# Ten early first-layer blocks ahead of the gates, six more kept in DRAM, channel transposes spread, x loaded in one row: a hybrid SSD and PEER layer

## The chip, the core and the metric

The kernel runs on one core of a Trainium2 chip. Times are device microseconds (us) of that core, and a kernel's time is the median of its runs. The engines are TensorE (PE, with its weight loads PEld), VectorE (DVE), ScalarE (ACT), GpSimd (POOL) and SyncE (SP), which issues most transfers.

## What is computed

One decoder layer over 512 tokens and 16 meta tokens of width 1024, in float32. The mixer is a projection into SSD and short-conv channels, and a product with an output matrix. Behind it stands the PEER block: 128 x 128 experts, 8 heads that choose 16 each.

```python
proj = n @ w_in                                  # z, xbc, dt, sc_b, sc_c, sc_x
xbc = silu(causal_dwconv(xbc, conv_ssd_w) + conv_ssd_b)
y = ssd_scan(xs, dt, A, Bm, Cm) + d_skip * xs    # chunks of 128 tokens
h = h + concat([rmsnorm(y * silu(z)), sc_b * causal_dwconv(sc_c * sc_x)]) @ w_out
n = rmsnorm(h)                                   # PEER
s = einsum('thsd,hskd->thsk', n @ w_q, sub_keys)
experts, gates = product_key_top16(s)            # per token and head
act = gelu(einsum('td,tkd->tk', n, expert_u[experts])) * gates
h = h + einsum('tk,tkd->td', act, expert_v[experts])
out = rmsnorm(h)[16:]
```

## The kernel before

All float32 products run as three passes over operands split into a high half (a ScalarE copy, line 88) and a low half (a subtraction, line 90, on VectorE or on GpSimd). `Stream` does this for all weights, in one order: a weight tile is loaded, then split piece by piece (two pieces to a block) four pieces ahead of use, in a ring of 12 halves.

**The first stage.** Rows of x are loaded in two pairs, normalised (`x_stats`), and transposed (`x_pair`); the first two projections begin on the first pair alone. Then 20 channel tiles are projected (`xbc_tile`: TensorE, an eviction by ScalarE, a convolution in four VectorE operations, a Silu). Of every four x tiles five chunks of tokens are transposed back (`to_tok`, four PSUM buffers), after the second projection of the next four.

**The experts.** The PEER block is computed densely for the last 384 tokens: for each of 128 blocks of 128 experts a first layer (`z_unit`, line 709, 24 matmuls and a Gelu) and a second layer (`vmm`, line 1036, 18 matmuls). What scales the result are gates, a 128 x 128 table for every token, which is built from one-hot products (`gates`, 24 calls of 32 small matmuls) and written to DRAM. `select` makes lists of experts out of the top-k; it casts the index lists on GpSimd (line 816), works on VectorE and has the three lists transposed by TensorE (line 871). The first 128 tokens gather their experts row by row (`fetch`, `dot`, `weigh`, `addv`) during the block loop.

First-layer blocks need no gates. So some are computed early: the first `NR` = 22 stay in SBUF, and those in `SPILL` are written to DRAM (`zd`) and read back in the block loop. `EARLYZ` lists both, `NZ0` counts them, `ZSEL` of them are issued ahead of the first `select`, `ZLATE` behind the last gate, and the rest are spread over the 24 gates calls. The block loop (`z_next`, `h_unit`, `sparse_step`, `vmm`) computes the others, 22 blocks ahead of use. `ZPOOL` says of how many early blocks GpSimd subtracts both low halves; `XP` says it for the channel projections, with its first entry for the first tile.

The code is written in this order, but a scheduler decides how the instructions stand on each engine. Every engine works its row in order.

Of the kernel before, what the change touches and what calls it, by code (L numbers as in the profile page):

```python
# [6 lines left out]
F32 = mybir.dt.float32  # L7
# [4 lines left out]
AF = mybir.ActivationFunctionType  # L12
# [5 lines left out]
P = 128  # L18
# [4 lines left out]
NT = T // P  # L23
L = META + T
NXS = 12
NG = 4
# [6 lines left out]
NB = 128  # L33
# [4 lines left out]
TC = 16  # L38
XP = ((False, True), (True, True))
ZLATE = 5  # L40
# [5 lines left out]
NR = 22  # L46
SPILL = tuple(range(NR + 2, NB - 6, 7))
EARLYZ = tuple(range(NR)) + SPILL
NZ0 = len(EARLYZ)
ZSEL = 6  # L50
ZPOOL = 6
NW = 12
# [64 lines left out]
def layer_kernel(tc, x, meta, g_mix, w_xbc, w_dt, w_sc, w_z, conv_w, conv_b, dt_bias, a_log, d_skip,  # L117
                 norm_w, sc_w, w_out, g_ffn, g_ffn_row, w_q, keys, u_t, uv, g_final, out, stage=99):
    nc = tc.nc
    dma = nc.sync.dma_start  # L120
    act = nc.scalar.activation
# [3 lines left out]
    with ExitStack() as top:  # L125
        const = top.enter_context(tc.tile_pool(name="const", bufs=1))
        dram = top.enter_context(tc.tile_pool(name="dram", bufs=1, space=DRAM))
        small = top.enter_context(tc.tile_pool(name="small", bufs=6))
        stp = top.enter_context(tc.tile_pool(name="stp", bufs=1))

        h = const.tile([P, NT, D], F32, name="h_in", tag="hbc")
# [9 lines left out]
        gmix = const.tile([P, KD], F32, name="gmix")  # L141
        gffn = const.tile([P, KD], F32, name="gffn")
        warm = small.tile([P, 1], F32, name="ss")
        nc.gpsimd.memset(warm, 1.0)
        act(warm, warm, AF.Sqrt)
        dma(out=meta_t, in_=meta)
        dma(out=h[:, 0, :], in_=x[0:P, :])
        dma(out=gmix, in_=g_mix)
        dma(out=h[:, 1, :], in_=x[P:2 * P, :])

# [32 lines left out]
        for g in range(NG):  # L183
            add(("xbc", 12 + g), w_xbc[12 + g], pool=XP[0 if g == 0 else 1])
            if g == 0:
                add(("dt",), w_dt, 1, KD * NH)
        for j in [16, 17, 18, 19] + list(range(NXS)):
            add(("xbc", j), w_xbc[j], pool=XP[1])
        for g in range(NG):
# [17 lines left out]
        st = Stream(nc, tc, stp, items)  # L207
        st.load_upto(2)
        for tt in range(2, NT):
            dma(out=h[:, tt, :], in_=x[tt * P:(tt + 1) * P, :])  # L210
        st.load_upto(4)
# [66 lines left out]

        x_stats(0)

        def x_pair(pr):
# [10 lines left out]
        x_pair(0)  # L292
        x_stats(1)

# [90 lines left out]
        xs_tok = [ring6(f"xs_tok{c}") for c in range(5)]  # L385
        b_tok = mc.tile([P, 4, NG, P], F32, name="b_tok")
        bc = const.tile([P, 2, NG, L], F32, name="bc", tag="hbc")
        b_ch = bc[:, 0]
# [12 lines left out]

        def to_tok(srcs, dst, nch=5):
            for c in range(nch):
                t0, t1 = tok(c)
                n = t1 - t0
                p = psS.tile([P, 512], F32, name="pS")
                for i, s in enumerate(srcs):
                    nc.tensor.transpose(p[:n, i * P:(i + 1) * P], s[:, t0:t1], ident)
                nc.any.tensor_copy(out=dst(c)[:n], in_=p[:n])

# [4 lines left out]
        for g in range(2):  # L415
            xbc_tile(16 + g, c_ch[:, g, :])
        to_tok([b_ch[:, g, :] for g in range(NG)], lambda c: b_tok[:, c].rearrange("p g n -> p (g n)"), 4)
        for g in range(2, NG):
            xbc_tile(16 + g, c_ch[:, g, :])
        do_dt3()  # L420
        pend = None
        for jg in range(3):
            srcs = []
            for i in range(4):
                xc = w2(L)
                xbc_tile(jg * 4 + i, xc)
                srcs.append(xc)
                if i == 1 and pend is not None:
                    pend()
            pend = lambda srcs=srcs, jg=jg: to_tok(srcs, lambda c: xs_tok[c][:, jg * 512:(jg + 1) * 512])  # L430

# [147 lines left out]
        def zb0():  # L579
            pend()  # L580
            for g in range(NG):
                ssd_a(0, g)
                ssd_b(0, g)
# [71 lines left out]
        h = const.tile([P, NT, D], F32, name="h", tag="hbc")  # L655
# [466 lines left out]
```

## Time and profile before

| | us |
|---|---|
| median of 3 runs (1717.19 to 1719.57) | 1719.07 |
| profiled execution | 1718.36 |
| span of its instructions | 1716.7 |
| TensorE busy | 1667.3 |
| VectorE busy | 1330.8 |
| ScalarE busy | 777.0 |
| GpSimd busy | 575.0 |

The stages, in us from the span's start: start and channel projections until 163, the rest of the mixer until about 475, the PEER queries until 575.7, the first `select` until 620, the gates until 771, remaining early blocks until 800, the block loop until 1708.5, the output until 1716.7. In the profile "L90" is line 90 of the kernel before; a wait stands in brackets behind the instruction that waited, with what released it.

### The profile page before, as it was taken

What the parts mean: (1) busy time and instruction counts of PE and PEld (TensorE: products, weight loads), DVE (VectorE), ACT (ScalarE), POOL (GpSimd) and SP (SyncE); (2) the same over time, 40 slices, a digit from 0 to 9 for tenths busy, and PEclk for the clock granted to TensorE, in tenths of its full rate; (3) what the DMA queues carried; (4) which work ended last, traced back from release to release, by engine and by line L of the source; (5) the groups of instructions that cost most, each with busy time, mean ns of one, the idle gap of its engine ahead of it and who ended that gap; (6) DMA issues with size and microseconds to landing.
All of it is one profiled execution on the core that took longest, in us unless ns stands there. A gap on an engine that the chain in (4) does not pass through costs nothing.

```text
span 1716.7 us, 26803 instructions
## 1 busy us (share of the span) xinstructions
PE 1667.3 (97%) x9544; PEld 1508.2 (88%) x9544; DVE 1330.8 (78%) x2820; ACT 777.0 (45%) x1548; POOL 575.0 (33%) x544
## 2 busy tenths in 40 slices
PE   6999999999999979999999999999999999999998
PEld 5989998878788978989999999999999999999886
DVE  5766468897689999995777777777777777777888
ACT  6444443455543445664444444444444444444444
POOL 2442335440155500202333333333333333333442
PEclk9999999999999989999999999999999999999999
DMA  4221221135532238889888887887888888888762
GB/s 153 75 84 56 73 98 50 65 98 199 180 99 84 90 116 251 257 269 372 320 301 304 328 325 287 331 319 290 327 311 311 310 317 314 317 300 330 274 240 99
DMA packets 131387, 382.91 MB, mean 223 GB/s; under 512 B 10532, under 2 KB 65444, under 8 KB 112820
## 3 DMA queue, kind: packets, MB, share of 16 engines
q1 hardware_dynamic: 112244, 245.92, 42.4%
q0 software_dynamic: 18432, 134.23, 20.3%
q8 instruction: 75, 1.23, 0.3%
q10 hardware_dynamic: 576, 1.05, 0.2%
q14 instruction: 60, 0.49, 0.1%
HBM read 351.14 MB, written 30.02 MB: 222 GB/s over the span
## 4 chain that ended last, share of the span: by engine, by line
PE 76%; DVE 18%; issue 3%; ACT 2%; DMA 0%; POOL 0%; SPq 0%; DVEq 0%; ACTq 0%; POOLq 0%
PE pV L1036 30%; PE pZ L709 26%; PE pA L303 6%; PE pA L600 5%; PE pA L443 4%; DVE w L399 2%; DVE o L912 2%; DVE w L90 1%; PE pR L918 1%; DVE o L908 1%; DVE x L774 1%; DVE x L771 1%; DVE ssb L772 1%; ACT w L88 1%; PE pS L532 1%
## 5 line engine op out<-in xcount | busy, mean ns | idle before, releaser
L88 ACT ACTIVATE w<-raw 128x512 fp32r<-128x512 f32 (+1 forms) x657 | 407.7, 625 | 611.3 <-PE pV L1036 243.8
L709 PE MATMUL pZ<-n,w 128*128 128x384 f32 (+1 forms) x3408 | 659.5, 347 | 0.0
L709 PEld LDWEIGHTS pZ<-n,w 128*128 128x128 f32 x3408 | 606.8, 189 | 21.4 <-DVE w L90 0.2
L90 POOL TENSOR_TENSOR w<-raw,w 128x512 fp32r<-128x512 f32 x211 | 292.0, 1390 | 754.5 <-ACT w L88 740.6
L1036 PE MATMUL pV<-w,hh 128*128 128x512 f32 x2304 | 537.2, 389 | 0.0
L90 DVE TENSOR_TENSOR w<-raw,w 128x512 fp32r<-128x512 f32 (+1 forms) x446 | 308.5, 694 | 252.7 <-ACT w L88 251.1
L1036 PEld LDWEIGHTS pV<-w,hh 128*128 128x128 f32 x2304 | 431.2, 188 | 82.7
L303 PE MATMUL pA<-nT,w 128*128 128x256 f32 (+3 forms) x1488 | 207.8, 296 | 0.6 <-ACT w L459 0.4
L303 PEld LDWEIGHTS pA<-nT,w 128*128 128x128 f32 (+1 forms) x1488 | 192.2, 188 | 5.4 <-ACT w L459 0.5
L969 DVE SCALAR_TENSOR_TENSOR h<-row,a,h 128x1024 f32<-128x1024 f32 x128 | 165.2, 1290 | 0.1
L959 DVE SCALAR_TENSOR_TENSOR row<-row,n2k 128x1024 f32<-128x1024 f32 x128 | 161.4, 1263 | 0.6 <-DMA row<-in_uv,xid 0.6
L953 POOL DMA_INDIRECT row<-in_uv,xid x128 | 144.8, 1132 | 23.3 <-DVE a L965 5.5
L1007 DVE TENSOR_TENSOR hh<-hf,hh 128x384 fp32r<-128x384 f32 x128 | 103.4, 808 | 20.0 <-ACT hh L1006 19.8
L506 POOL TENSOR_TENSOR sr<-aS,ut 128x384 fp32r<-128x384 f32 x64 | 66.5, 1059 | 79.9 <-PE pS L508 41.5
L1004 DVE TENSOR_TENSOR hf<-zg,gt 128x384 f32<-128x384 f32 x128 | 81.3, 635 | 5.1 <-DMA gt<-gd 1.4
L1006 ACT ACTIVATE hh<-hf 128x384 fp32r<-128x384 f32 x128 | 65.5, 512 | 33.0 <-PE pV L1036 18.5
L921 ACT ACTIVATE stg<-pR 128x512 f32<-128x512 f32 x96 | 54.4, 599 | 39.3 <-PE pR L918 26.2
L443 PE MATMUL pA<-w,nT 128*128 128x384 f32 x384 | 72.2, 345 | 0.0
L443 PEld LDWEIGHTS pA<-w,nT 128*128 128x128 f32 x384 | 68.6, 192 | 1.6 <-issue 1.1
L788 ACT ACTIVATE zg<-pZ 128x384 f32<-128x384 f32 x128 | 61.0, 477 | 19.7 <-PE pZ L709 18.7
L918 PE MATMUL pR<-o,o 128*128 128x128 f16 x768 | 58.0, 222 | 6.1 <-DVE o L912 6.1
L912 DVE TENSOR_TENSOR o<-oag,ob 128x1024 f16<-128x1024 f16 x96 | 63.3, 695 | 0.0
(235 smaller groups left out, 1421.8 us busy)
## 6 DMA issues: line engine op xcount, KB each, us to landing
raw<-in_u_t SPq DMA_DIRECT2D x128, 512.0 KB, 4.8
raw<-in_uv SPq DMA_DIRECT2D x128, 512.0 KB, 4.9
gd<-stg SPq DMA_DIRECT2D x24, 1024.0 KB, 6.4
gt<-gd SPq DMA_DIRECT2D x16, 1536.0 KB, 9.8
raw<-in_w_out SPq DMA_DIRECT2D x32, 512.0 KB, 3.5
raw<-in_w_xbc SPq DMA_DIRECT2D x20, 512.0 KB, 3.5
raw<-in_w_q SPq DMA_DIRECT2D x16, 512.0 KB, 3.5
raw<-in_w_z SPq DMA_DIRECT2D x16, 384.0 KB, 3.0
```

What stands on the lines that cost most here:

```text
L88: nc.scalar.activation(hi, r, AF.Copy)
L90: ins = (nc.gpsimd if on_pool else nc.vector).tensor_tensor(lo, r, hi.bitcast(F32), ALU.subtract)
L303: mm(p[:m, :o1 - o0], wp[a][:, c0:c0 + m], nTs[b][:, k, o0:o1], start=i == 0, stop=i == 3 * KD - 1)
L443: mm(pz[tt][:, :GW], nTs[b][:, k, t0:t0 + P], wz[a], start=k == 0 and i == 0, stop=k == KD - 1 and i == 2)
L600: mm(po[pr, i, nh], ys[b], wp[a], start=kn == 0 and q == 0, stop=kn == 15 and q == 2)
L709: mm(ps[s][:, :o1 - o0], wp[a_][:, k * P:(k + 1) * P], n2s[b_][:, 4 * i + k, o0:o1], start=cnt[s] == 0, stop=cnt[s] == 23)
L912: V.tensor_tensor(o1, oag[:, t0 // 2:t0 // 2 + 2, :, None, :].broadcast_to([P, 2, 16, 16, 2]), ob[:, t0 // 2:t0 // 2 + 2, None, :, :].broa ...
L953: nc.gpsimd.indirect_dma_start(out=row.rearrange("p a d -> p (a d)"), out_offset=None, in_=uv, in_offset=bass.IndirectOffsetOnAxis(ap=xids ...
L959: V.scalar_tensor_tensor(row[:, 0], row[:, 0], 1.0, n2k[:, tt], ALU.mult, ALU.mult, accum_out=z)
L969: V.scalar_tensor_tensor(h[:, tt, :], row[:, 1], a, h[:, tt, :], ALU.mult, ALU.add)
L1007: V.tensor_tensor(hl, hf_, hh.bitcast(F32), ALU.subtract)
L1036: mm(acc[tt, nh], hp_[a][:, ts_], vp_[w], start=b == 0 and q == 0, stop=b == NB - 1 and q == 2)
```

## The change

`SPILL` takes every fifth block instead of every seventh: 20 blocks instead of 14 are kept in DRAM, 42 instead of 36 are early. `ZSEL` and `ZPOOL` go from 6 to 10. The rest of the early blocks (27 for 25) is spread over the gates, five come behind them. `to_tok` takes a list of chunks and is called three times, with two, two and one chunk, after the first, second and third projection of the next four tiles; its copies go to ScalarE, where the scheduler chose between two engines before. All four loads of x come ahead of the first weights, and both `x_stats` stand in one row. The first tile's first low half moves to GpSimd, and a Sqrt that did nothing but load ScalarE's table is gone. Line numbers of the new file are 5 lower from the middle on.

```diff
-XP = ((False, True), (True, True))
+XP = ((True, True), (True, True))
...
-SPILL = tuple(range(NR + 2, NB - 6, 7))
+SPILL = tuple(range(NR + 2, NB - 6, 5))
 EARLYZ = tuple(range(NR)) + SPILL
 NZ0 = len(EARLYZ)
-ZSEL = 6
-ZPOOL = 6
+ZSEL = 10
+ZPOOL = 10
...
-        warm = small.tile([P, 1], F32, name="ss")
-        nc.gpsimd.memset(warm, 1.0)
-        act(warm, warm, AF.Sqrt)
         dma(out=meta_t, in_=meta)
-        dma(out=h[:, 0, :], in_=x[0:P, :])
-        dma(out=gmix, in_=g_mix)
-        dma(out=h[:, 1, :], in_=x[P:2 * P, :])
+        for tt in range(NT):
+            dma(out=h[:, tt, :], in_=x[tt * P:(tt + 1) * P, :])
+            if tt == 0:
+                dma(out=gmix, in_=g_mix)
...
         st = Stream(nc, tc, stp, items)
-        st.load_upto(2)
-        for tt in range(2, NT):
-            dma(out=h[:, tt, :], in_=x[tt * P:(tt + 1) * P, :])
         st.load_upto(4)
...
         x_stats(0)
+        x_stats(1)
...
         x_pair(0)
-        x_stats(1)
...
-        def to_tok(srcs, dst, nch=5):
-            for c in range(nch):
+        def to_tok(srcs, dst, chunks):
+            for c in chunks:
...
-                nc.any.tensor_copy(out=dst(c)[:n], in_=p[:n])
+                act(dst(c)[:n], p[:n], AF.Copy)
...
-                if i == 1 and pend is not None:
-                    pend()
-            pend = lambda srcs=srcs, jg=jg: to_tok(srcs, lambda c: xs_tok[c][:, jg * 512:(jg + 1) * 512])
+                if i < 3 and pend is not None:
+                    pend((2 * i, 2 * i + 1)[:5 - 2 * i])
+            pend = lambda ch, srcs=srcs, jg=jg: to_tok(srcs, lambda c: xs_tok[c][:, jg * 512:(jg + 1) * 512], ch)
...
-            pend()
+            pend(range(5))
```

TensorE between the last query and the first gate, before. `pZ` with 384 columns is a first-layer block (24 matmuls), the line 871 transposes the lists, and `o` are one-hot factors:

```order
L765 MATMUL pR<-kt,qT 128x128 x4
L709 MATMUL pZ<-n_4669,w 128x384 x138
L871 MATMUL pR<-ident,lists 128x128 x3
L709 MATMUL pZ<-n_4669,w 128x384 x44
L918 LDWEIGHTS o_6749
L918 MATMUL pR<-o_6751,o_6749 128x128
```

And now:

```order
L760 MATMUL pR<-kt,qT 128x128 x4
L704 MATMUL pZ<-n_4666,w 128x384 x234
L866 MATMUL pR<-ident,lists 128x128 x3
L704 MATMUL pZ<-n_4666,w 128x384 x44
L913 LDWEIGHTS o_6894
L913 MATMUL pR<-o_6896,o_6894 128x128
```

Of first-layer matmuls 96 more, four blocks, stand ahead of the lists' transposes; behind them there are 44 as before.

GpSimd at the same place, before; `cand` are sums of candidates, `xT` is the cast of index lists and line 90 the subtraction of a low half:

```order
L90 TENSOR_TENSOR w<-raw,w 128x512
L733 TENSOR_TENSOR cand<-v_2_5090 128x64
L733 TENSOR_TENSOR cand<-v_3_5091 128x48
L733 TENSOR_TENSOR cand<-v_3_5091 128x64
L816 CAST xT<-x_1_5093 128x256
L90 TENSOR_TENSOR w<-raw,w 128x512 x4
L816 CAST xT<-x_2_5094 128x256
L816 CAST xT<-x_3_5095 128x256
L816 CAST xT<-x_0_5092 128x256
```

And now:

```order
L728 TENSOR_TENSOR cand<-v_2_5087 128x64
L728 TENSOR_TENSOR cand<-v_3_5088 128x48
L728 TENSOR_TENSOR cand<-v_3_5088 128x64
L811 CAST xT<-x_1_5090 128x256
L90 TENSOR_TENSOR w<-raw,w 128x512 x5
L811 CAST xT<-x_2_5091 128x256
L90 TENSOR_TENSOR w<-raw,w 128x512 x7
L811 CAST xT<-x_3_5092 128x256
L811 CAST xT<-x_0_5089 128x256
L862 COPY xg_6449<-lists 128x128
```

Four subtractions between the first and the second cast have become five, and seven stand between the second and the third.

VectorE's row at the start, before. The 16-row operations are the meta tokens' norm; `w,ss<-h_in` squares half a row of x:

```order
L265 SCALAR_TENSOR_TENSOR w_151,ss_146<-h_in 128x512
L225 RECIPROCAL rs_r<-rs_t 16x1
L265 SCALAR_TENSOR_TENSOR w_153,ss_146<-h_in 128x512
L226 TENSOR_TENSOR rs_t<-rs_r 16x1
L90 TENSOR_TENSOR w<-raw,w 128x512
L227 TENSOR_TENSOR rs_t<-rs_t,rs_v 16x1
L270 TENSOR_TENSOR ss_155<-ss_146 128x2
L228 TENSOR_SCALAR rs_t<-rs_t 16x1
L223 TENSOR_SCALAR rs_v<-ss_155 128x2
L229 TENSOR_TENSOR rs_r<-rs_r,rs_t 16x1
L240 TENSOR_SCALAR mn<-meta_t,rs_r 16x1024
L225 RECIPROCAL rs_r<-rs_t 128x2
```

And now:

```order
L260 SCALAR_TENSOR_TENSOR w_148,ss_143<-h_in 128x512
L220 RECIPROCAL rs_r<-rs_t 16x1
L260 SCALAR_TENSOR_TENSOR w_150,ss_143<-h_in 128x512
L221 TENSOR_TENSOR rs_t<-rs_r 16x1
L260 SCALAR_TENSOR_TENSOR w_171,ss_166<-h_in 128x512
L222 TENSOR_TENSOR rs_t<-rs_t,rs_v 16x1
L265 TENSOR_TENSOR ss_152<-ss_143 128x2
L260 SCALAR_TENSOR_TENSOR w_173,ss_166<-h_in 128x512
L223 TENSOR_SCALAR rs_t<-rs_t 16x1
L218 TENSOR_SCALAR rs_v<-ss_152 128x2
L265 TENSOR_TENSOR ss_175<-ss_166 128x2
L224 TENSOR_TENSOR rs_r<-rs_r,rs_t 16x1
```

The first low half is gone from it. Of two more squares (of the fourth row of x) one stands ahead of the first pair's sums (`ss_152`), one ahead of the variance (`rs_v`) made of them.

## Rows read from the trace of the kernel before

**Rows 1.** The page, part 1: busy time, share of the span, count of instructions.

```profile
PE 1667.3 (97%) x9544; PEld 1508.2 (88%) x9544; DVE 1330.8 (78%) x2820; ACT 777.0 (45%) x1548; POOL 575.0 (33%) x544
```

**Rows 2.** Busy us (count) of PE, PEld, DVE, ACT, POOL; granted clock, DMA share, GB/s.

```profile
600.20:620.00 19.80, 10.40 (x48) 9.65 (x47) 19.34 (x62) 2.99 (x7) 2.68 (x1) 0.83 0.25 80
...
620.00:771.10 151.10, 147.91 (x1307) 136.08 (x1306) 147.56 (x264) 95.89 (x176) 14.61 (x3) 0.98 0.81 240
...
800.20:1708.50 908.30, 908.30 (x4490) 818.12 (x4488) 690.37 (x1099) 382.67 (x798) 323.11 (x253) 1.00 0.82 301
```

**Rows 3.** Waits of TensorE, the longest: total us, times, longest.

```profile
PE pS L286 <- DVE rs_r L225: 12.9, 1, 12.9
```

**Rows 4.** Timeline, TensorE, ahead of the gates: start us, us, operation, [idle before, releaser].

```profile
575.71 24.62 PE L709 MATMUL pZ<-n,w 128*128 128x384 f32 x138
...
605.62 0.47 PE L871 MATMUL pR<-ident,lists 128*128 128x128 f32 x1 [5.19 <-DVE lists L854]
...
607.55 9.56 PE L709 MATMUL pZ<-n,w 128*128 128x384 f32 x44
...
620.01 0.62 PE L918 MATMUL pR<-o,o 128*128 128x128 f16 x8 [2.90 <-DVE o L912]
```

**Rows 5.** Timeline, TensorE, projections of the first stage.

```profile
80.61 35.37 PE L303 MATMUL pA<-nT,w 128*128 128x272 f32 x288
...
121.94 0.65 PE L408 MATMUL pS<-ident,w 128*128 128x128 f32 x4 [4.21 <-DVE xs_tok L409]
...
150.78 0.66 PE L408 MATMUL pS<-ident,w 128*128 128x128 f32 x4 [1.49 <-ACT xs_tok L409]
...
162.96 2.28 PE L443 MATMUL pA<-w,nT 128*128 128x384 f32 x12
```

**Rows 6.** One line's matmuls, L709 then L1036 twice: PE busy (count), PEld busy, clock.

```profile
800.20:1620.00 819.80, 400.81 (x2186) 387.80 (x2184) 1.00 0.85 314
...
800.20:1620.00 819.80, 448.64 (x1915) 358.08 (x1916) 1.00 0.85 314
1620.00:1708.60 88.60, 88.51 (x391) 72.96 (x389) 1.00 0.50 179
```

**Rows 7.** Timeline, GpSimd, ahead of the gates and in them.

```profile
587.11 0.65 POOL L816 CAST xT<-x 128x256 f16<-128x256 uint32 x1
...
587.73 5.11 POOL L90 TENSOR_TENSOR w<-raw,w 128x512 fp32r<-128x512 f32 x4
...
602.33 2.68 POOL L816 CAST xT<-x 128x256 f16<-128x256 uint32 x1 [9.49 <-DVE oh L851]
...
685.73 9.74 POOL L816 CAST xT<-x 128x256 f16<-128x256 uint32 x1 [53.08 <-DVE oh L851]
```

**Rows 8.** The page, part 5: the costliest groups.

```profile
L90 DVE TENSOR_TENSOR w<-raw,w 128x512 fp32r<-128x512 f32 (+1 forms) x446 | 308.5, 694 | 252.7 <-ACT w L88 251.1
```

**Rows 9.** Timeline, ScalarE, projections of the first stage.

```profile
108.26 0.74 ACT L400 ACTIVATE w<-w,cb__105 128x528 f32<-128x528 f32 x1 [4.23 <-DVE w L399]
...
114.82 0.74 ACT L400 ACTIVATE w<-w,cb__105 128x528 f32<-128x528 f32 x1 [4.23 <-DVE w L399]
```

**Rows 10.** Timeline of the start, several engines.

```profile
7.83 0.69 DVE L265 SCALAR_TENSOR_TENSOR w<-h_in 128x512 f32<-128x512 f32 x1 [3.04 <-DMA h_in<-in_x]
...
9.11 1.15 ACT L88 ACTIVATE w<-raw 128x512 fp32r<-128x512 f32 x2 [2.70 <-DMA raw<-in_w_xbc]
...
10.34 1.26 POOL L90 TENSOR_TENSOR w<-raw,w 128x512 fp32r<-128x512 f32 x1 [8.04 <-ACT w L88]
...
10.38 1.23 DVE L227 TENSOR_TENSOR rs_t<-rs_t,rs_v 16x1 f32<-16x1 f32 x1
...
13.17 0.16 DVE L227 TENSOR_TENSOR rs_t<-rs_t,rs_v 128x2 f32<-128x2 f32 x1
...
15.33 1.97 PE L251 MATMUL pS<-ident,hn 128*128 128x128 f32 x8 [1.45 <-DVE hn L277]
...
26.83 1.33 PE L251 MATMUL pS<-ident,hn 128*128 128x128 f32 x8 [0.99 <-DVE hn L277]
```

More of the change, by code (lines that the diff above doesn't have):

```diff
@@ L416, in layer_kernel @@
             xbc_tile(16 + g, c_ch[:, g, :])
-        to_tok([b_ch[:, g, :] for g in range(NG)], lambda c: b_tok[:, c].rearrange("p g n -> p (g n)"), 4)
+        to_tok([b_ch[:, g, :] for g in range(NG)], lambda c: b_tok[:, c].rearrange("p g n -> p (g n)"), range(4))
         for g in range(2, NG):
```

## The prediction

> **What bounds the kernel now.** I read the page first. TensorE is busy for 97% of the span [rows 1], but that is an average over stages, so the stretches are next [rows 2]. From 800 us on TensorE has no gap at a full clock for 908 us: a block costs there what its matmuls cost. Between 600.2 and 620.0 it is busy for 10.4 of 19.8 us at a granted clock of 0.83, and in the gate stage (620.0 to 771.1) VectorE is busy for 147.6 of 151.1 us and TensorE for 147.9, at 0.98. The longest of TensorE's waits is the first, 12.9 us before any transpose [rows 3]; the timelines add 5.2 us for the first expert lists and 2.9 for the first one-hot products [rows 4], and 4.2 and 1.5 us in the channel transposes [rows 5]. The change works on these places, so each is taken by itself.
>
> **A matmul's price.** Ahead of the gates 138 first-layer matmuls take 24.5 us from 575.71 until the lists are wanted at 600.2 [rows 4], 0.177 us each. In the block loop 391 second-layer matmuls take 88.6 us, 0.2266 each; 1915 of them make 434 of the 819.8 us before, and what is left over 2186 first-layer matmuls is 0.1765 us [rows 6]. A block of the first layer is 24 of them, 4.24 us.
>
> **1. The loop gives 25.4 us back.** Before, 14 blocks beyond the first 22 are computed early and kept in DRAM; now 20. Six blocks leave the loop: 144 x 0.1765 = 25.4 us. TensorE sets the pace there without a gap [rows 2], and VectorE, busy for 690 of 908 us, loses twelve subtractions with it. Six loads of 192 KB come for six of 512 KB that go, so the transfers, at a mean share of 0.82, shrink. A step without a first-layer block is 18 x 0.2266 = 4.1 us on TensorE; up to the last 22 such steps come every fifth time, never two in a row, and VectorE catches up between them. I take the whole 25.4, with 24 as the lower end.
>
> **2. In front of the gates: +9.2 us.** Four more blocks stand ahead of the transposes of the first lists (234 matmuls in one row in place of 138), and 44 matmuls behind them as before: 96 x 0.177 = 17.0 us more work. What it can fill: 19.8 us, less 44 x 0.177 = 7.8 and some 0.6 for the three transposes (an estimate; the row of one shows 0.47 with its drain), so 11.4 us. If nothing else waited, the first gate would move by 5.6 us. The lists no longer hold TensorE up: the ones that came at 605.6 are there long before it asks, at 575.7 + 234 x 0.177 = 617.2.
>
> But a new wait appears. The low halves of blocks 6 to 9 are now subtracted on GpSimd, and its row has the second cast of indices (line 816) after five of the twelve subtractions that follow the first cast. That cast waits for VectorE and starts at 602.33 [rows 7]; seven subtractions, for pieces 13 to 19 (two to a block, counted from 0), stand behind it. TensorE reaches piece 13 after 156 matmuls, six of which are done at 575.7: 575.7 + 150 x 0.177 = 602.3, and its third matmul, at 602.7, wants the low half. The cast takes 2.68 us there and a subtraction 5.11 / 4 = 1.28, so the low half is ready at 606.3: a wait of 3.6 us. Later pieces come every 1.28 us against 2.13 on TensorE and wait no more. The four casts of the trace take from 0.65 to 9.74 us; with these ends the wait is 1.6 or 10.7. I take the row of the same place. Sum: 17.0 - 11.4 + 3.6 = +9.2, between +7.2 and +16.3.
>
> **3. Gate stage: +5.5 us.** Two more blocks lie between the first and the last gate, 48 x 0.1765 = 8.5 us on TensorE, and five more subtractions on VectorE (49 for 44 in its row) at 0.69 us [rows 8], 3.5 us. VectorE has 3.5 us free in the stage and TensorE 3.2 [rows 2]. On TensorE the lower clock costs 0.02 x 151 = 3.0 us; it follows the hole ahead of it, which the change fills. I give the stage these 3.0 back: +5.5. The ends are +2.3 (the 3.2 us of gaps go as well; VectorE's 147.6 + 3.5 = 151.1 would still fit) and +8.5 (nothing comes back).
>
> **4. Channel transposes: +0.5 us, no gain.** The two waits (4.2 and 1.5 us) come when TensorE wants a fifth transposed chunk and the first has not been copied. Spread over three projections, no fifth one comes. But TensorE is ahead of the chain behind it there. Six projections take 35.4 us from 80.61, 5.9 each [rows 5]; the chain of eviction, convolution and Silu takes 114.82 - 108.26 = 6.56 us for each [rows 9]. The first group now stands one projection earlier, at 80.6 + 5 x 5.9 = 110.1, and needs the Silu that ends at 114.82 + 0.74 = 115.6: a wait of 5.5 us in place of 4.2. From there TensorE has two sets of five chunks (0.65 us for four transposes with their drain, some 0.5 without, 2.5 a set: my estimate) and seven projections, 41.3 us: 115.6 + 5.0 + 41.3 = 161.9, where the next stage starts at 162.96 in the trace. So the wait moves, and 1 us is gained. If the clock falls after it as it did at 607.55, 1.8 us are lost. I take +0.5, between -1.5 (the second wait goes whole) and +2.
>
> **5. Start: +2.0 us.** All four loads of x now go ahead of the first weights, the statistics of both pairs run in one row, and both halves of the first weights are subtracted on GpSimd. Against: VectorE's two squares of the fourth row of x stand ahead of the first pair's variance. Rows of 512 KB land 1.3 us apart here (x at 7.83, weights at 9.11) [rows 10], so that row lands near 7.8 + 2 x 1.3 = 10.4, and the variance follows two squares of 0.69 later, near 11.9. Then the weights' subtractions on GpSimd, now four in one row, fall into VectorE's row of small operations. The trace shows what that does: the multiplication of line 227 takes 1.23 us beside a subtraction on GpSimd (10.34 to 11.6) and 0.16 without one, on more elements. Four of these are 4.3 us at most, and none is 0; I take 3.5 for the start of the pair's transposes, from 15.33 to 18.8. For: the second pair's statistics are there when the first is done, so TensorE's gap of 0.99 us at 26.83 goes, with some 0.5 at the evictions behind it. Net +2.0, between -1.0 and +3.6. The Sqrt that warmed the table is gone, so one more table load stands in ScalarE's row; it falls into its wait for x and costs nothing.
>
> The Trainium skill bears on this ("SBUF — State Buffer", section "Who interferes with whom"): GpSimd and VectorE share one pair of ports, and whoever starts first holds it for the whole instruction. The row of 1.23 us agrees. Were the lock to hold for all four subtractions one after the other, the start would cost 4 x 1.28 - 1.5 = +3.6 instead of +2.0 and the sum would be -6.6.
>
> **Sum.** +2.0 + 0.5 + 9.2 + 5.5 - 25.4 = -8.2 us. The profiled execution took 1718.36 us (span 1716.7), which gives 1710.2; the median of the three runs, 1719.07, is 0.7 above it, which gives 1710.9. I say **1711**.
>
> **Rivals.**
> *A. What is gained in the loop is spent ahead of it.* The start at its upper end, +3.6; after the wait for the cast the clock falls again as it did (the 44 matmuls took from 607.55 until 617.1, 1.8 us over their price); the gate stage at +8.5. Then 3.6 + 0.5 + 9.2 + 1.8 + 8.5 - 25.4 = -1.8: 1717. For it: both engines are full in that stage. Against: the lower clock there has a cause that goes. It is no change that can be measured: some 0.2%, 3.4 us, is what runs of this kernel can tell.
> *B. Slower: the second cast takes as long as the longest of its kind.* At 9.74 us, pieces 13 to 19 come 7.1 us later still: front +16.3, 1.8 for the clock behind it, gate stage +8.5, and 2.0 + 0.5 - 25.4: +3.7, or 1723. From a cast of 6 us on the change no longer pays. For it: the cast's time hangs on how densely VectorE works beside it. Against: in this very place it took 2.68.
> *C. The transposes' waits do go,* because the Silu is not what the first group waits for: -5.7 instead of +0.5, sum -14.4: 1705. Against: the times of the chain above. Only then would the spreading do there what it says.
>
> **How the numbers follow.** Forecast 0.60, A 0.17, B 0.09, C 0.14. Faster by over 0.2%: the forecast and C, 0.74; within it: A, 0.17; slower: B, 0.09. The ends of the five terms, all on one side, would reach from 1701 to 1725; they hang on different causes, and most of the forecast lies from 1704 to 1716. The range of 8 in 10 goes from below C, 1703, to above A, 1719, and leaves out B and the outermost edges.
>
> **What would show it.** Right: the first one-hot product near 629 us; a wait of TensorE for GpSimd's line 90 of 2 to 4 us near 602 and none for the lists; a granted clock of 1.0 in the first gates; 2040 first-layer matmuls in a loop of some 883 us; a wait for a Silu near 112 us; the first pair's transposes near 19 us. Wrong: a wait of 10 us near 602, a gate stage of 160 us or more, gaps of TensorE in the loop, or channel transposes without any wait.

## Result and the profile after

The changed kernel takes 1709.01 us, median of five runs (1708.16 to 1710.60). The kernel before took 1717.57 us beside it (five runs, 1717.19 to 1719.57). The ratio is 0.9948, 95% interval 0.9934 to 0.9963: faster by 8.6 us, 0.5%. The forecast was 1711, between 1703 and 1719. Run again on another occasion, the changed kernel took 1710.87 us against 1717.83, ratio 0.9959 (0.9945 to 0.9972). Both say the same; the gain is 7 to 9 us. Two executions among the runs below, of 3606.17 us (the start alone) and 2050.42 us (the casts on VectorE), far slower than all others, stand in no median and no ratio.

The profiled execution of after took 1709.91 us with a span of 1708.2, 8.5 us less than the span of before. Its lines have moved up by five behind the loads of x (line 303 before is 298 now, 709 is 704, 816 is 811, 918 is 913), and by four at line 286, now 282. The page, part 1, stands against [rows 1]: TensorE is busy for 4.6 us less, VectorE and GpSimd for 15.5 and 22.8 us more.

```profile
PE 1662.7 (97%) x9544; PEld 1506.9 (88%) x9544; DVE 1346.3 (79%) x2806; ACT 778.7 (46%) x1552; POOL 597.8 (35%) x552
```

The windows that answer to [rows 2]: in front of the gates, the gate stage, the loop. Columns: stretch, its length, busy us (count) of TensorE, its weight loads, VectorE, ScalarE, GpSimd, then granted clock, DMA share, GB/s.

```profile
579.82:632.35 52.53, 49.13 (x285) 48.59 (x284) 50.75 (x178) 23.20 (x40) 22.91 (x26) 1.00 0.36 121
```

```profile
632.35:786.39 154.04, 150.43 (x1324) 141.95 (x1322) 150.91 (x268) 96.21 (x178) 21.73 (x3) 0.99 0.85 253
```

```profile
817.50:1700.00 882.50, 882.50 (x4345) 792.55 (x4343) 697.92 (x1085) 373.13 (x780) 330.81 (x253) 1.00 0.83 308
```

The hole of 9.4 us between 600 and 620 is gone, the clock stays at 1.00 there, and the loop, still without a gap of TensorE, is 882.5 us long in place of 908.3. The waits of TensorE (us in total, times, longest) have changed as follows: those for copies of the transposes (line 409 before, [rows 5]) have become one for a Silu, the longest of those for the lists [rows 4] is gone, and one for GpSimd's line 90 is new.

```profile
PE pS L403 <- ACT w L395: 5.3, 3, 4.8
PE pS L246 <- DVE hn L272: 4.9, 1, 4.9
PE pZ L704 <- POOL w L90: 3.4, 1, 3.4
...
PE pS L567 <- DVE ysz L563: 2.4, 3, 1.9
```

TensorE's timeline at the places of [rows 5] and [rows 4] (start, length, operation, count, idle time before it and who ended it):

```profile
82.69 29.51 PE L298 MATMUL pA<-nT,w 128*128 128x272 f32 x240
...
117.32 1.24 PE L403 MATMUL pS<-ident,w 128*16 128x128 f32 x5 [4.79 <-ACT w L395]
...
163.76 2.24 PE L438 MATMUL pA<-w,nT 128*128 128x384 f32 x12
```

```profile
579.82 26.60 PE L704 MATMUL pZ<-n,w 128*128 128x384 f32 x152
609.81 14.48 PE L704 MATMUL pZ<-n,w 128*128 128x384 f32 x82 [3.40 <-POOL w L90]
...
624.37 8.02 PE L704 MATMUL pZ<-n,w 128*128 128x384 f32 x44
632.35 0.62 PE L913 MATMUL pR<-o,o 128*128 128x128 f16 x8
```

To see where the time went, the span is cut at five places that every kernel here has: the first projection of the row of six (80.61 us before), the first product of the next stage (162.96), the last product of keys ahead of the gates (574.79), the first one-hot product (620.01), the first second-layer product of the loop (800.22), and the end of the span. A column of this table is how much longer or shorter a piece is than in the trace of before, in us; each row is one profiled execution.

| kernel | start | transposes | 163 to 575 | front of gates | gates | loop | span |
|---|---|---|---|---|---|---|---|
| predicted | +2.0 | +0.5 | 0 | +9.2 | +5.5 | -25.4 | -8.2 |
| the changed kernel | +2.1 | -1.3 | +3.3 | +8.2 | +4.9 | -25.7 | -8.5 |
| the changed kernel, again | +1.8 | +0.2 | +4.7 | +8.3 | +4.9 | -25.6 | -5.8 |
| start's edits only | +1.8 | +0.5 | +0.9 | -0.1 | -0.1 | 0.0 | +2.9 |
| transposes only | 0.0 | -0.4 | +0.9 | -0.1 | +0.2 | 0.0 | +0.6 |
| blocks only | -0.4 | -0.1 | 0.0 | +10.9 | +5.9 | -25.7 | -9.4 |
| blocks and transposes | -1.3 | -1.3 | +1.8 | +9.7 | +5.1 | -25.7 | -11.6 |
| changed, casts on VectorE | +1.6 | +0.2 | +4.7 | +8.7 | +4.8 | -25.7 | -5.8 |
| changed, six blocks in front | +2.1 | +0.1 | +1.2 | -0.1 | +22.0 | -25.7 | -0.4 |
| changed, fourteen in DRAM | +2.9 | -1.0 | +1.5 | +10.1 | -9.1 | 0.0 | +4.3 |
| blocks, transposes later | -1.7 | -6.3 | +6.9 | +9.8 | +6.1 | -25.8 | -11.0 |
| blocks, transposes, casts on VectorE | +0.8 | -0.3 | -0.3 | +8.9 | +7.1 | -25.8 | -9.6 |
| changed, first weights as before | +1.9 | +0.2 | +1.3 | +8.2 | +5.9 | -25.7 | -8.2 |
| eleven, transposes later, casts on VectorE | -1.2 | -6.3 | +6.9 | +11.1 | +1.0 | -25.7 | -14.2 |

The largest difference from the forecast is a piece that the change doesn't touch: 163 to 575 us. There the granted clock falls in the output projection. The windows of TensorE's wait for `ysz` and of what follows, of before and then of after:

```profile
375.00:377.00 2.00, 1.42 (x9) 1.08 (x8) 2.00 (x5) 0.74 (x2) 0.00 (x0) 1.00 0.39 160
377.00:383.00 6.00, 6.00 (x28) 5.00 (x27) 5.97 (x11) 3.91 (x8) 2.96 (x3) 1.00 0.36 111
```

```profile
375.00:377.00 2.00, 1.65 (x11) 1.44 (x12) 2.00 (x6) 1.09 (x2) 0.00 (x0) 0.77 0.80 238
377.00:383.00 6.00, 5.99 (x17) 4.52 (x16) 5.21 (x11) 1.82 (x4) 0.83 (x1) 0.51 0.28 96
```

For six microseconds after does 17 matmuls where before does 28: TensorE is at 1.2 GHz, half its clock. What came before it is a wait of 1.9 us (1.5 in before).

### The profile page after: what moved, and what is told of

The parts are those of the page before. It is cut to its first block, busy times and chain, and to the rows that moved or that the text cites. A ratio compares the mean times of both kernels' runs of the same rounds, so it can differ in the third digit from the quotient of the medians.

```text
span 1708.2 us, 26849 instructions
## 1 busy us (share of the span) xinstructions
PE 1662.7 (97%) x9544; PEld 1506.9 (88%) x9544; DVE 1346.3 (79%) x2806; ACT 778.7 (46%) x1552; POOL 597.8 (35%) x552
## 4 chain that ended last, share of the span: by engine, by line
PE 82%; DVE 14%; issue 1%; ACT 1%; DMA 0%; POOL 0%; SPq 0%; ACTq 0%; POOLq 0%; DVEq 0%
PE pV L1031 30%; PE pZ L704 28%; PE pA L298 10%; PE pA L595 4%; PE pA L438 4%; PE pR L913 2%; DVE o L907 1%; DVE x L769 1%; DVE x L766 1%; DVE ssb L767 1%; PE pS L527 1%; DVE v L768 1%; DVE v L765 1%; DVE w L394 1%; DVE w L90 1%
## 5 line engine op out<-in xcount | busy, mean ns | idle before, releaser
L704 PE MATMUL pZ<-n,w 128*128 128x384 f32 (+1 forms) x3408 | 649.5, 345 | 3.4 <-POOL w L90 3.4
L90 POOL TENSOR_TENSOR w<-raw,w 128x512 fp32r<-128x512 f32 x220 | 310.6, 1419 | 716.8 <-ACT w L88 712.4
L90 DVE TENSOR_TENSOR w<-raw,w 128x512 fp32r<-128x512 f32 (+2 forms) x437 | 304.1, 700 | 211.8 <-ACT w L88 210.1
L1002 DVE TENSOR_TENSOR hh<-hf,hh 128x384 fp32r<-128x384 f32 x128 | 113.7, 888 | 25.7 <-ACT hh L1001 25.4
L394 DVE SCALAR_TENSOR_TENSOR w<-w,cw,w 128x528 f32<-128x528 f32 x60 | 56.9, 948 | 1.8
```

What stands on the lines that cost most here:

```text
L90: ins = (nc.gpsimd if on_pool else nc.vector).tensor_tensor(lo, r, hi.bitcast(F32), ALU.subtract)
L704: mm(ps[s][:, :o1 - o0], wp[a_][:, k * P:(k + 1) * P], n2s[b_][:, 4 * i + k, o0:o1], start=cnt[s] == 0, stop=cnt[s] == 23)
L1002: V.tensor_tensor(hl, hf_, hh.bitcast(F32), ALU.subtract)
```

## The experiments

**The start alone.** The edit (with the warming Sqrt taken away as well):

```diff
-XP = ((False, True), (True, True))
+XP = ((True, True), (True, True))
...
-        dma(out=h[:, 0, :], in_=x[0:P, :])
-        dma(out=gmix, in_=g_mix)
-        dma(out=h[:, 1, :], in_=x[P:2 * P, :])
+        for tt in range(NT):
+            dma(out=h[:, tt, :], in_=x[tt * P:(tt + 1) * P, :])
+            if tt == 0:
+                dma(out=gmix, in_=g_mix)
...
-        st.load_upto(2)
-        for tt in range(2, NT):
-            dma(out=h[:, tt, :], in_=x[tt * P:(tt + 1) * P, :])
         st.load_upto(4)
...
         x_stats(0)
+        x_stats(1)
...
         x_pair(0)
-        x_stats(1)
```

> Only the edits of the start: all loads of x ahead of the first weights, both statistics in one row, no warming Sqrt, four subtractions of the first weights on GpSimd. If the terms of the sum stand by themselves, the six projections' row starts 2 us later than before (82.7 instead of 80.6) and the end moves by the same 2.0 us: 1719.6. Rival: the dip of the granted clock at 361 to 401 us, which the changed kernel shows and the kernel before does not, comes with the later start; then the output projection loses some 2.9 us more and the end moves by 4.9. Second rival: the wait in the channel transposes takes the 2 us up, and the end moves by 0 to 0.5.

1720.37 us against 1718.39, ratio 1.0012 (1.0003 to 1.0022): +2.1 us by the ratio. The row of projections starts 1.8 us later. The clock falls in the output projection here too (0.50 and 0.60 in the two windows above), so the dip came with this edit; that it need not is seen below. It costs 2.3 us in this trace (the first rival had 2.9), but 1.6 us come back between 163 and 271 us, where the clock from 165 to 200 us is 1.00 and not 0.95. So the +2.1 us are not the start's cost alone.

**The transposes alone.**

```diff
-                nc.any.tensor_copy(out=dst(c)[:n], in_=p[:n])
+                act(dst(c)[:n], p[:n], AF.Copy)
...
-                if i == 1 and pend is not None:
-                    pend()
+                if i < 3 and pend is not None:
+                    pend((2 * i, 2 * i + 1)[:5 - 2 * i])
```

> Only the spreading of the channel transposes, their copies on ScalarE. Term 4 as predicted: +0.5 us, with a wait of TensorE for a Silu near 110 us of some 5.5 us and no other there. By the two traces compared: -1.3, with a wait of 4.8 us. Rival C: the waits of 4.2 and 1.5 us go and nothing takes their place, -5.7. If the dip of the clock at 361 to 401 us comes with this edit, 2.9 us are to be added to each.

1717.52 us against 1718.39, ratio 0.9997 (0.9988 to 1.0006): no difference that can be measured. TensorE's two waits for copies (4.2 and 1.5 us) are replaced by one of 5.04 us for the Silu. Rival C is out: the waits don't go. The run doesn't separate the spreading from the copies on ScalarE.

**The blocks alone.**

```diff
-SPILL = tuple(range(NR + 2, NB - 6, 7))
+SPILL = tuple(range(NR + 2, NB - 6, 5))
...
-ZSEL = 6
-ZPOOL = 6
+ZSEL = 10
+ZPOOL = 10
```

> Only the blocks: ten ahead of the first gates, twenty beyond the first 22 kept in DRAM, the subtractions of blocks 6 to 9 on GpSimd. The terms add: +9.2 in front of the gates, +5.5 in the gate stage, -25.4 in the loop, together -10.7 us as predicted; with the sizes of the two traces compared (+8.2, +5.1, -25.7) -12.4. TensorE waits 2 to 4 us for GpSimd near 606 us and never for the lists. Rival: the dip of the clock at 361 to 401 us belongs to this edit although it lies ahead of the place that is edited (the trace then shows the dip here, and the sum is -9.5); otherwise the output projection takes as long as before.

1709.03 us, ratio 0.9942 (0.9929 to 0.9956): -10.0 us by the ratio, against -10.7 by the three terms. The whole gain of the change lies in these three numbers. By ratios the three parts add up to 2.1 - 0.5 - 10.0 = -8.4 us.

**Blocks and transposes, the start undone.** The edits of the two runs above.

> The blocks and the transposes, with the start as it was. If the terms add, this is the changed kernel less what the start costs: 2.0 us less by the prediction, so some 1707, with the six projections' row at 80.6 us again. If the dip of the clock in the output projection also goes away with the start's edits, 4.9 us less: 1704. Rival: the start's cost is taken up by a later wait, and the time is that of the changed kernel, 1709.

1708.20 us, ratio 0.9941 (0.9927 to 0.9954): -10.1 us, as the blocks alone. By the ratios the kernel is 1.2 to 3.1 us better without the start's edits, but the intervals overlap, so between the forecast here (1707) and its rival (1709) this run doesn't decide. The single trace shows more (-11.6).

Here the clock in front of the gates can be compared. The 82 matmuls behind the wait for GpSimd (3.4 us in each of the three traces) take 14.5, 16.0 and 17.2 us, in the changed kernel, in blocks and transposes, and in blocks alone; the clock is the third number from the right.

```profile
609.81:624.30 14.49, 14.49 (x84) 14.46 (x85) 13.63 (x41) 5.02 (x10) 7.84 (x6) 1.00 0.55 172
```

```profile
604.89:620.90 16.01, 16.01 (x84) 15.97 (x85) 13.79 (x41) 4.98 (x10) 7.81 (x6) 0.89 0.55 177
```

```profile
605.15:622.30 17.15, 17.15 (x83) 17.12 (x84) 13.75 (x41) 4.94 (x10) 7.77 (x6) 0.84 0.56 183
```

One and the same wait is followed by no loss, by 1.5 us or by 2.7 us. That alone makes up the difference between +8.2 and +10.9 in the table's column.

**The cast that GpSimd waits in, moved away.** The changed kernel with

```diff
-        nc.gpsimd.tensor_copy(xT, x16.rearrange("p (h s) x -> p s x h", s=2))
+        (nc.gpsimd if tt == order[0] else V).tensor_copy(xT, x16.rearrange("p (h s) x -> p s x h", s=2))
```

> The changed kernel with every index cast but the first on VectorE instead of GpSimd, so that GpSimd's twelve subtractions stand in one row and the wait of TensorE for its line 90 (3.40 us at 609.81 in the changed kernel) can't come. If that wait is what term 2 lost, TensorE's 234 matmuls run through and the first one-hot product comes 3.4 us earlier, 628.9 instead of 632.35; three casts of some 0.4 to 0.7 us more in VectorE's row cost the gate stage at most 2. Net -1.4 to -3.4 against the changed kernel: 1705.6 to 1707.6. Rival: VectorE ends last there (it is busy for 19.9 of the 20 us from 600 to 620) and the wait is only taken over by one for the lists or the one-hot products: 0, or up to 2 us slower.

1712.62 us, ratio 0.9965 (0.9952 to 0.9978): no gain. The interval overlaps both of the changed kernel's, and the trace is that of its second execution: +6.5 and +6.7 us ahead of 575 us, where nothing was edited, and front and gates within half a microsecond. TensorE's timeline ahead of the gates:

```profile
582.22 40.81 PE L704 MATMUL pZ<-n,w 128*128 128x384 f32 x234
...
625.45 7.55 PE L704 MATMUL pZ<-n,w 128*128 128x384 f32 x42 [1.75 <-DVE w L90]
635.18 0.62 PE L913 MATMUL pR<-o,o 128*128 128x128 f16 x8 [2.18 <-DVE o L907]
```

The 234 matmuls run through, as the theory had it. But then TensorE waits 1.75 and 2.18 us for VectorE, 3.9 in place of 3.4: from the first of these matmuls to the first one-hot product it is 52.96 us in place of 52.53. Part of this is the edit's own doing: counted from the first of these matmuls, VectorE's last list is complete after 40.0 us here and after 38.2 in the changed kernel. But in the changed kernel, too, VectorE is busy for 50.75 of the 52.53 us (window above), and its first one-hot factor is complete at 632.30 us, just ahead of 632.35. So the wait for GpSimd had cover: of its 3.4 us at most 1.8 could be gained without taking work off VectorE.

**The same without the start's edits.** Edits of the blocks, the transposes and the cast.

> The blocks and the transposes with the start as it was, and the index casts but the first on VectorE. If both gains stand by themselves, 1708.2 (blocks and transposes) less the 1.4 to 3.4 of the wait: 1704.8 to 1706.8. Rival as for the run before: the wait is taken over by VectorE, 1708 or more.

1708.79 us, ratio 0.9942 (0.9930 to 0.9955), against 0.9941 without the cast's edit. Waits of 1.19 and 2.18 us for VectorE stand in place of that for GpSimd. In the traces the front is 0.9 us shorter by the edit and the gate stage 2.0 longer. The rival holds in both kernels.

**The six more blocks through the gates only.** The changed kernel with

```diff
-ZSEL = 10
-ZPOOL = 10
+ZSEL = 6
+ZPOOL = 6
```

> The changed kernel with six blocks ahead of the gates as before, twenty kept in DRAM: the six more blocks all go through the gate stage, and the hole ahead of the gates (11.4 us by term 2) is not filled. The loop gives the same 25.4 back. If TensorE sets the gate stage once six blocks more are in it (144 x 0.1765 = 25.4 us against 3.2 us of gaps and 3.0 us of lower clock), the stage gets 19 to 25 us longer and the time is 0 to 6 us below before's with the start's 2 us on top: 1713 to 1720. Rival: the stage is VectorE's and takes more blocks for little (twelve subtractions at 0.69, +8.3): then front 0, gates +8.3, loop -25.4, start and transposes +0.8: 1702.

1716.38 us, ratio 0.9994 (0.9985 to 1.0003). The loop gives the same 25.7 us back, and the gates take 22.0 of it. The window of this kernel from the first one-hot product to the last:

```profile
623.33:794.52 171.19, 167.19 (x1418) 160.17 (x1418) 156.98 (x276) 102.63 (x190) 12.53 (x3) 0.98 0.80 242
```

TensorE is busy for 167.2 us and VectorE for 157.0: TensorE sets this stage. Six blocks moved out of the loop, 25.7 us there, cost 22 in the gates.

**Ten blocks in front, but only fourteen in DRAM.** The changed kernel with

```diff
-SPILL = tuple(range(NR + 2, NB - 6, 5))
+SPILL = tuple(range(NR + 2, NB - 6, 7))
```

> The changed kernel with only fourteen blocks kept in DRAM as before, but ten ahead of the gates: the loop gives nothing back and the gate stage has four blocks less than before (96 x 0.1765 = 16.9 us of TensorE). In front +8.2 as in the changed kernel. If VectorE sets the stage then, it loses only the subtractions of these blocks (at most eight at 0.69, 5.5 us): +8.2 - 5.5 and the start's and the transposes' +0.8 = +3.5 against before, 1721 to 1722. If TensorE sets it, -16.9: -8, 1710.

1721.03 us, ratio 1.0020 (1.0011 to 1.0029): 2.9 us slower than before, as the first theory had it. The same window, of before and then of this kernel:

```profile
620.01:768.98 148.97, 145.79 (x1274) 134.17 (x1273) 145.43 (x260) 94.02 (x172) 14.61 (x3) 0.98 0.81 239
```

```profile
633.45:777.45 144.00, 135.07 (x1204) 120.99 (x1202) 141.92 (x254) 89.01 (x162) 16.94 (x3) 0.98 0.79 237
```

Here VectorE is busy for 141.9 of 144.0 us and TensorE for 135.1: VectorE sets it. Three of the four blocks come out of this window (461 recorded first-layer matmuls for 532), 12.7 us of TensorE's work, and shorten it by 5.0 us only. The fourth comes out of the stretch between the last one-hot product and the loop (145 for 169), where it gives its whole 4.2 us. So the two halves of the block edit need each other: filling the hole pays as long as the gates get enough blocks to fill TensorE beside VectorE, and blocks from the loop pay as far as there is a hole to put them in.

**The transposes one projection later.** Blocks and transposes, start undone, and

```diff
-                if i < 3 and pend is not None:
-                    pend((2 * i, 2 * i + 1)[:5 - 2 * i])
+                if i and pend is not None:
+                    pend((2 * i - 2, 2 * i - 1)[:7 - 2 * i])
```

> Blocks and transposes with the start as it was, and the spread transposes each one projection later (behind the second, third and fourth projection of the next group instead of the first three). By term 4's account the first group then stands at 80.6 + 6 x 5.9 = 116.0, behind the Silu that ends at 115.6: the wait of 5 us goes, and as the chain of eviction, convolution and Silu (6.56 us a projection against 5.9 on TensorE) comes back only 0.7 us a projection, the next stage starts some 4 us earlier, at 156 to 157 instead of 160.4: 1704 to 1705. Rival: the chain sets that whole row of projections, the wait comes back as one for its evictions or at the next stage, and the time stays at that of blocks and transposes, 1708.2.

1706.13 us, ratio 0.9929 (0.9916 to 0.9943). Against 0.9941 for the same without this edit that would be 2 us, but the intervals overlap. The trace shows both theories, one after the other. TensorE's timeline:

```profile
78.88 36.89 PE L303 MATMUL pA<-nT,w 128*128 128x272 f32 x288
115.61 1.03 PE L408 MATMUL pS<-ident,w 128*16 128x128 f32 x8
...
154.89 1.29 PE L443 MATMUL pA<-w,nT 128*128 128x384 f32 x6
157.91 0.79 PE L443 MATMUL pA<-w,nT 128*128 128x384 f32 x3 [1.73 <-ACT w L395]
159.01 0.79 PE L443 MATMUL pA<-w,nT 128*128 128x384 f32 x3 [0.31 <-ACT w L395]
...
163.39 0.61 PE L408 MATMUL pS<-ident,w 128*16 128x128 f32 x4 [1.24 <-ACT w L400]
```

The wait for the Silu is gone, and the next stage begins at 154.89 instead of 160.36, 5.5 us earlier (0.4 of it stood at the row of six already). There ScalarE is behind, and three waits (1.73, 0.31 and 1.24) give 3.3 us back. From 165 to 200 us the clock is at 0.90 and not at 0.95. At 206 us only 0.4 us of the 5.5 are left in this trace.

**The changed kernel once more.**

> The changed kernel once more. If the dip of the granted clock in the output projection (0.88 and 0.95 from 360.8 to 400.8 us, 2.9 us) belongs to where the start's edits put this stage, it is there again; if it is one draw of many, it is gone or stands at another place, and the times scatter by 1 to 3 us with the mean clock, 0.991 to 0.995. Median 1708 to 1710 either way.

1710.87 us (1708.19 to 1713.18), as given above. The dip of the clock in the output projection is there again (0.95 and 0.88 in the two windows of 20 us from 360.8, where it was 0.88 and 0.95), and a further one lies between 165 and 200 us (0.90 for 0.95).

**The first weights as before.** The changed kernel with `XP = ((False, True), (True, True))`.

> The changed kernel with the first half of the first weights subtracted on VectorE as before, so that three and not four subtractions stand on GpSimd in the start. Term 5 put 3.5 us of the later start of the pair's transposes (18.7 instead of 15.3) down to these and to the two squares ahead of the variance. If GpSimd's row is what the pair waits for, the transposes start 1 to 1.3 us earlier, near 17.5, and the end moves with them. Rival: the squares and the load of the fourth row of x hold the pair up, and one subtraction more on VectorE makes it 0 to 0.7 us later.

1710.62 us beside 1710.87 for the changed kernel: nothing. The pair's transposes start at 19.04 us, not earlier; the square that waits for a load of x stands 0.6 us later in this trace (10.71 for 10.10 us), so the edit itself gave some 0.25 us at most. The start of the changed kernel, and then of this one (VectorE, GpSimd and TensorE; the rows are of three timelines):

```profile
11.53 0.15 DVE L218 TENSOR_SCALAR rs_v<-ss 128x2 f32<-128x2 f32 x1
...
15.35 1.14 DVE L222 TENSOR_TENSOR rs_t<-rs_t,rs_v 128x2 f32<-128x2 f32 x2
```

```profile
12.13 3.01 POOL L90 TENSOR_TENSOR w<-raw,w 128x512 fp32r<-128x512 f32 x2 [9.87 <-ACT w L88]
...
15.14 2.48 POOL L90 TENSOR_TENSOR w<-raw,w 128x512 fp32r<-128x512 f32 x2
```

```profile
18.68 1.97 PE L246 MATMUL pS<-ident,hn 128*128 128x128 f32 x8 [4.87 <-DVE hn L272]
```

```profile
12.14 0.15 DVE L218 TENSOR_SCALAR rs_v<-ss 128x2 f32<-128x2 f32 x1
...
14.02 1.19 DVE L218 TENSOR_SCALAR rs_v<-ss 128x2 f32<-128x2 f32 x1
...
15.36 1.21 DVE L221 TENSOR_TENSOR rs_t<-rs_r 128x2 f32<-128x2 f32 x1
...
17.91 0.16 DVE L221 TENSOR_TENSOR rs_t<-rs_r 128x2 f32<-128x2 f32 x1
```

One instruction of VectorE on two elements a partition takes 0.15 us, and 1.2 us while GpSimd subtracts (13.34 to 17.78 us in the second kernel). With three subtractions GpSimd starts 1.2 us later and as many of VectorE's small operations still meet it; the one subtraction that VectorE gets is 0.69 us more.

**Eleven blocks in front.** The kernel with later transposes, the casts on VectorE, and `ZSEL = 11`, `ZPOOL = 11`.

> As two runs before (start as it was, blocks, transposes one projection later), with the later index casts on VectorE and an eleventh block ahead of the gates. With the casts there, TensorE waited 1.2 and 2.2 us for VectorE in front of the first gates; a block is 4.24 us, so it nearly fits: the first one-hot product comes 0.9 us later than with ten, and the gate stage, which has a block less, gets 0 to 4.2 us shorter, as VectorE sets it or TensorE. 0 to 3.4 us below the run with the casts on VectorE (1708.8), and less by what the later transposes give: 1701 to 1708. Rival: VectorE gets later by the block's subtraction (0.7 us) and by its port, the hole stays, and nothing is gained: 1709 less the transposes' part.

1703.67 us (1702.39 to 1705.14), ratio 0.9918 (0.9904 to 0.9931): 14 us faster than before, and the interval lies clear of both of the changed kernel's. It is the best of the kernels here. Its timeline ahead of the gates, and its gate stage:

```profile
575.05 45.82 PE L709 MATMUL pZ<-n,w 128*128 128x384 f32 x258
...
630.46 0.62 PE L918 MATMUL pR<-o,o 128*128 128x128 f16 x8 [1.64 <-DVE o L912]
```

```profile
630.46:780.66 150.20, 146.14 (x1299) 135.60 (x1298) 149.31 (x268) 94.64 (x175) 16.85 (x1) 1.00 0.83 253
```

With 24 matmuls more (4.24 us by the price of the prediction) the front is 55.41 us long where the same kernel without the eleventh block and without the later transposes has 53.19 (575.91 to 629.10). The gate stage, which has a block less, takes 150.2 us for 156.05 there; the clock is 1.00 for 0.99. VectorE, at 149.3 of 150.2 us, has nothing left to give. In the traces front and gates together cost +12.1 us here, +16.0 with the casts alone and +14.9 in blocks and transposes, while ahead of 575 us the three stand within 1 us of each other. No run tells the eleventh block from the later transposes, and the interval overlaps that of blocks and transposes (0.9927 to 0.9954).

## Why the prediction was right, and where it was not

**1. The loop.** Right: -25.7 in the trace against -25.4, and -25.6 to -25.8 in every kernel that keeps twenty blocks in DRAM, 0.0 in those with fourteen. No gap of TensorE came.

**2. Front of the gates.** The sum held, +8.2 against +9.2, and the new wait came where it was placed and nearly as long: 3.40 us for 3.6, behind the first 152 matmuls of that row. GpSimd's timeline in the changed kernel, against [rows 7]:

```profile
591.77 6.36 POOL L90 TENSOR_TENSOR w<-raw,w 128x512 fp32r<-128x512 f32 x5
607.47 0.61 POOL L811 CAST xT<-x 128x256 f16<-128x256 uint32 x1 [9.34 <-DVE oh L846]
608.05 9.61 POOL L90 TENSOR_TENSOR w<-raw,w 128x512 fp32r<-128x512 f32 x7
```

There is luck in the size, since errors cancel. The cast took 0.61 us and not 2.68; but it started 1.0 us later against the row of TensorE, since it waits for VectorE (9.34 us), and the first subtraction behind it took 1.71 us and not 1.28.

What failed is the account of the hole. It was made on TensorE alone: 11.4 us to fill, so +5.6 without a wait. VectorE had no hole. The window of the front of before, and that of the run with the casts on VectorE; the changed kernel's stands above:

```profile
575.71:620.01 44.30, 34.89 (x189) 34.08 (x187) 43.84 (x180) 16.50 (x28) 14.23 (x18) 0.92 0.30 95
```

```profile
582.22:635.18 52.96, 49.03 (x284) 48.46 (x283) 52.55 (x181) 23.06 (x40) 23.17 (x25) 1.00 0.35 119
```

VectorE is busy for 43.84 of 44.30 us before and for 50.75 of 52.53 in the changed kernel, with as many instructions (180 and 178): 6.9 of the +8.2 us are its longer busy time. [Rows 2] had the sign of it, 19.34 of 19.80 us. GpSimd has eight instructions more there (26 for 18), and VectorE's are longer where they meet its subtractions. In the changed kernel one operation stands twice, in GpSimd's idle time and beside its row of seven:

```profile
603.57 0.42 DVE L848 TENSOR_TENSOR oh<-oh 128x512 f16<-128x512 f16 x1
...
609.83 1.51 DVE L848 TENSOR_TENSOR oh<-oh 128x512 f16<-128x512 f16 x1
```

Term 5 priced this for the start; term 2 put it at nothing. With the wait for GpSimd taken away the front stayed as long, with VectorE busy for 52.55 of 52.96 us. Whether the low halves of blocks 6 to 9 had better stayed on VectorE (eight subtractions at 0.69, 5.5 us, an estimate) no run shows: each with ten blocks in front has them on GpSimd.

**3. Gate stage.** +4.9 in the table (+5.1 between the first and the last one-hot product) for +5.5, with the clock at 0.99 for 0.98. The two runs on the number of blocks show why the term had bounds on both sides: with six blocks more than before between the first and the last one-hot product TensorE sets the stage, with three less VectorE does, and as it stands both are full (150.4 and 150.9 of 154.0 us).

**4. Channel transposes.** "No gain" was right, by the mechanism that was given: the wait goes to the Silu (4.79 us at 117.32, for 5.5). The size was off in the first trace, -1.3 for +0.5, and not in the second, +0.2. Most of the difference is the clock behind the wait, for which the working named 1.8 us: the next 48 matmuls took 6.91 and 8.20 us, where such a row takes 6.07. The edit alone moved the time by less than can be measured. The account ended at the next stage, though. The run with later transposes shows that it goes on: the chain of eviction, convolution and Silu is behind there too, and takes back what TensorE gains ahead of it.

**5. Start.** +2.1 and +1.8 for +2.0, and +2.1 us timed with this edit alone. The pair's transposes start at 18.68, forecast 18.8; of these 3.4 us, 1.3 come back at the gap of [rows 10]. The Trainium skill ("SBUF — State Buffer", section "Who interferes with whom") has VectorE and GpSimd share a pair of ports that is held for a whole instruction; the rows of 1.2 us beside 0.15 agree. The +3.6 that the lock would have made of the start did not come. Which of the start's edits costs the 2 us no run shows, other than that the first low half does not.

**The step that was missing.** The sum took the piece from 163 to 575 us as unchanged, as if a stage that starts 1 us later ran as before. It cost +3.3 us (in the second execution +4.7). Counted at the transposes of `ysz` on either side, 2.4 and 2.3 us of it are the clock after a wait for `ysz`, 0.5 in each that wait itself (1.9 us for 1.5), and 0.4 and 1.9 lie ahead of it, in the second with the clock at 0.90 from 165 to 200 us. That the sum came out at -8.2 for a span of -8.5 is therefore partly luck: this loss stands against 1.8 us less at the transposes and some 2 us less in the other terms. The working gave no price to a clock that falls behind waits that were there before.

What decides whether the clock falls there stays open. All traces with the start's edits show the dip (0.85 to 0.95 from 360.8 to 380.8), so a shift of 1 to 4 us seemed to be the cause; but without these edits it is in four traces (0.91 from 360.8 to 380.8, among them blocks and transposes and the best kernel) and missing in three (before, transposes only, blocks only), and blocks only reaches the wait for `ysz` 0.6 us earlier than before, the run with the casts on VectorE and no start's edits 0.7 us earlier. Nor does the length of that wait decide: 1.46 us is followed by no dip in before and in blocks only and by one in the start's edits only, 1.92 by none in transposes only and by one in blocks and transposes. One profiled execution of each kernel can't tell a fixed relation from chance. No run put a delay alone in front of an unchanged kernel.

Rival B (a long cast) is excluded by the row of 0.61 us, rival C by the run of the transposes alone. Rival A's price for a lower clock behind the wait for GpSimd did come in other kernels (16.0 and 17.2 us for the 82 matmuls), not in the two traces of the changed one.

The forecast of 1711 stood on 1719.07, the median of three runs; from the 1717.57 of five the same sum gives 1709.4, beside 1709.01 measured.

## What to carry over

Work moved to an earlier stage gains the idle time that it fills there, and no more: six blocks out of the loop gave 25.7 us in each case, and by the ratios the net ran from -10.0 us (hole and gates both filled) to -1.0, within the noise (gates only, with the start's 2 us in it). A hole of one engine is room only if the others have one there too: VectorE was full where TensorE waited, and the subtractions given to GpSimd made its instructions longer. Before a wait is taken away, look at what the engine would wait for next: of the two that were taken away here, the one for GpSimd came back in full as waits for VectorE, and 3.3 of the 5 us of the one for the Silu as waits for ScalarE. A difference of 1 to 3 us between two traces can be the clock alone, so cut both spans at the same places of the program and read each piece's granted clock before giving it to an edit.

## What the chip showed

- After a wait of 1.9 us TensorE went on at 1.2 GHz (0.51 from 377 to 383 us in the changed kernel); after one as long, in the run of the transposes alone, the clock stayed at 1.00. After the same 3.4 us of wait it was 1.00, 0.89 or 0.84 over the next 82 matmuls. The Trainium skill ("TensorE: Matmul & The Clock Gate", section "Part 1: The HAM clock gate") says that the gate's clockwork runs free of the program, so that a kernel has more or fewer slow matmuls from run to run. The two traces of the changed kernel (0.95 and 0.90 from 165 to 200 us) agree, and so does the spread of the kernel before, 1716.04 to 1720.29 us over the runs shown with the experiments, with a mean clock from 0.990 to 0.995.
- Beside a row of GpSimd subtractions of 128 x 512 elements, VectorE's operations on two elements a partition took up to 1.2 us, and 0.15 otherwise; one on 512 elements took 1.51 us, and 0.42 otherwise.
